# The scaling of differential attention's output, five copies of the embedding product, and the last gate's tile, moved in a two-layer encoder trunk

## The chip, the core and the metric

The kernel runs on one core of one Trainium2 chip. The metric is the device time of one execution in microseconds (us). TensorE is called PE below, its weight loads PEld, VectorE DVE, ScalarE ACT, GpSimd POOL, and SyncE, which issues the DMAs, SP.

## What is computed

A two-layer encoder over 1024 tokens of width 1024, float32. Layer 0 mixes tokens by neighbourhood attention, layer 1 by dense differential attention; each layer then has a gated feed-forward part and adds a sigmoid-gated embedding. Cut to what matters here:

```python
# layer 1, per head h and block of 128 queries
s = einsum('bhmqd,bhmkd->bhmqk', qb, k) + bias[None, :, None]   # two maps m = 0, 1
a = softmax(s, axis=-1)
w = a[:, :, 0] - lam_full * a[:, :, 1]
o = einsum('bhqk,bhkd->bhqd', w, v)
...
o = rms_norm(o, subln_g) * (1.0 - lambda_init)
...
# the end of each layer
gate = sigmoid(rms_norm(x, g[4]) @ ple_w_gate[i])
x = x + gate * (p[i] @ ple_w_proj[i])
```

## The kernel before, in words

Every float32 product is made of three matmuls of float32r parts (high by high, high by low, low by high). PE's order is written by hand. Only the differential attention (`da`) and the end of layer 1 are touched by the change.

**Differential attention.** There are 64 steps: 8 heads with 8 blocks of 128 queries. A turn `n` of the loop in `da` (L1193) issues on PE, in this order: the values of step n-1 (`da_values`, L1143), the scores of step n+1 for both maps (`da_scores`, L1088), the transposes of the weights of step n in two halves (`da_turn`, L1129), and the transpose of the scaled output of step n-1 (`da_out`, L1160). Between these, `tick` draws matmuls from a second stream (`da_stream`): the projections of later heads (L286 to L288), then the embedding product (`embed_steps`, L2146), then two blocks of the output projection (L1379).

Inside this loop the order of ACT, DVE and POOL is written by hand too: they run what the program issues, in that order. The chain beside PE for step n+1 is: DVE adds the bias to the scores of map 0 and takes the row's minimum (`biased`, L1099), then the same for map 1; ACT takes the exponential of map 0 and of map 1 (`da_exp`, L1106), each needing its minimum; DVE joins the two maps to weights (`da_weights`, L1113 to L1116); PE transposes these in the next turn, and ACT copies each half out of PSUM (L1132). For step n-1, whose values PE has just made, ACT squares and sums the output (L1146), DVE adds epsilon (L1147), POOL takes the power -0.5 (`root`, L298), and DVE scales the output by it (L1152), which PE then transposes (L1160). The tile `os` that the scaling writes has one buffer.

The second stream takes its PSUM banks from a pool of two (`take`, L611). The embedding product makes 16 tiles of 128x512; each is copied out of its bank by ACT (`evict`, L2154) and sent to DRAM by SP (L2155). PE can begin the next tile but one only when the copy has freed the bank. The copies are issued where `tick` happens to draw the tile's last unit: behind the exponential of map 0 (L1211), of map 1, or at the end of the turn.

**The last gate.** `embed` (L1998) makes, for each of 8 blocks of tokens, the product with `ple_w_gate` (24 matmuls of 128x512 for each half of 512 columns), and `gate` (L2025) takes the sigmoid on ACT (L2031), multiplies by the embedding and adds it to the residual on DVE (L2032, L2033), and sends the result off (L2034). For the last block of layer 1 PE makes one half after the other, and `gate` handles both halves after that. Both lie in one tile `g` of two banks.

## Time and profile before

| what | value |
|---|---|
| time, median of 3 runs | 2694.28 us (2693.45 to 2697.17) |
| the profiled execution's own time | 2693.09 us |
| its span, first to last instruction | 2691.3 us |
| PE busy | 2655.9 us, 99% |
| DVE, ACT, POOL busy | 1966.0, 1382.3, 549.4 us |
| granted TensorE clock | 1.00 |
| differential attention | about 1310 to 1885 us |

Durations below come from that one execution. Matmuls are pipelined: a matmul of 128x512 is shown 0.39 us long, though the next one starts 0.23 us later, so what counts on PE is the distance of the starts. A wait of an engine is shown as idle time before an instruction with the one that released it.

### The profile page before, as it was taken

The page shows a single profiled execution, that of the slowest core. Times are in us where ns is not written, and L with a number is a line of the kernel's source. Part 1 is how long each engine was busy: PE and PEld are TensorE (multiplying, and loading weights), DVE is VectorE, ACT ScalarE, POOL GpSimd, SP SyncE. Part 2 cuts the span into 40 slices and gives each one's busy share as a digit, 9 for nine tenths or more (in the row PEclk, how much of TensorE's full clock was granted, in tenths as well). Part 3 has the DMA queues.
Part 4 walks back from the last instruction along what each step waited for, and adds up shares of the span by engine and source line. Part 5 has one row for each costly group of instructions (what it writes and reads, how often), then busy time and mean ns, then how long its engine had stood idle before and what let it go on. Part 6 is the DMA issues. An engine that isn't in the chain of part 4 may idle for free.

```text
span 2691.3 us, 37010 instructions
## 1 busy us (share of the span) xinstructions
PE 2655.9 (99%) x13384; PEld 2195.3 (82%) x13384; DVE 1966.0 (73%) x3369; ACT 1382.3 (51%) x2612; POOL 549.4 (20%) x526
## 2 busy tenths in 40 slices
PE   8999999999999999999999999999999999999999
PEld 6888887878888888888778888877878888888887
DVE  5777776699777768666577777775798777767674
ACT  5555556454444444454466666675454343444452
POOL 2221220003333301001542122210103433300000
PEclk9999999999999999999999999999999999999999
DMA  6223226423322273343346555552413232373342
GB/s 185 85 66 105 77 94 192 136 67 122 118 101 111 91 277 137 110 130 121 123 155 211 202 174 200 180 180 92 157 65 142 84 117 94 122 262 123 117 138 101
DMA packets 150937, 360.91 MB, mean 134 GB/s; under 512 B 14137, under 2 KB 41017, under 8 KB 150754
## 3 DMA queue, kind: packets, MB, share of 16 engines
q1 hardware_dynamic: 150754, 358.56, 39.7%
q8 instruction: 105, 1.72, 0.3%
q14 instruction: 78, 0.64, 0.1%
HBM read 277.79 MB, written 92.90 MB: 138 GB/s over the span
## 4 chain that ended last, share of the span: by engine, by line
PE 84%; DVE 6%; ACT 3%; DMA 3%; issue 2%; POOL 1%; SPq 0%; DVEq 0%; ACTq 0%; POOLq 0%
PE b L286 19%; PE b L287 19%; PE b L288 19%; PE g L1379 6%; PE m L1379 5%; PE b L1143 3%; PE s L1088 3%; PE b L1129 2%; PE b L317 2%; PE b L1379 2%; PE av L981 2%; PE b L954 1%; DMA r<-in_ffn_w_out 1%; DVE r L252 1%; ACT E L1106 1%
## 5 line engine op out<-in xcount | busy, mean ns | idle before, releaser
L286 PE MATMUL b<-r,ws 128*128 128x512 f32 (+1 forms) x1308 | 532.8, 407 | 2.5 <-DVE r L421 1.8
L288 PE MATMUL b<-r,ws 128*128 128x512 f32 (+1 forms) x1308 | 506.2, 387 | 0.6 <-DVE ws L252 0.6
L287 PE MATMUL b<-r,ws 128*128 128x512 f32 (+1 forms) x1308 | 505.5, 386 | 0.7 <-DVE r L252 0.5
L288 PEld LDWEIGHTS b<-r,ws 128*128 128x128 f32 x1308 | 246.1, 188 | 53.1 <-DVE ws L252 1.8
L286 PEld LDWEIGHTS b<-r,ws 128*128 128x128 f32 x1308 | 246.8, 189 | 50.4 <-issue 3.3
L287 PEld LDWEIGHTS b<-r,ws 128*128 128x128 f32 x1308 | 247.6, 189 | 34.9 <-DVE r L252 1.9
L298 POOL TENSOR_TENSOR ss<-ss,mhalf 128x1 f32<-128x1 f32 x128 | 77.7, 608 | 953.8 <-DVE ss L1147 426.3
L286 PE MATMUL b<-r,wa 128*128 128x512 f32 x688 | 268.3, 390 | 2.0 <-DVE B L1772 2.0
L288 PE MATMUL b<-r,wa 128*128 128x512 f32 x688 | 268.2, 390 | 0.0
L287 PE MATMUL b<-r,wa 128*128 128x512 f32 x688 | 267.9, 389 | 0.0
L286 PE MATMUL b<-r,r 128*128 128x512 f32 x648 | 254.5, 393 | 1.0 <-ACT ws L2143 0.6
L287 PE MATMUL b<-r,r 128*128 128x512 f32 x648 | 252.9, 390 | 0.4 <-DVE r L252 0.3
L288 PE MATMUL b<-r,r 128*128 128x512 f32 x648 | 252.6, 390 | 0.0
L249 ACT ACTIVATE r<-raw 128x512 fp32r<-128x512 f32 (+1 forms) x168 | 109.0, 656 | 193.7 <-PE b L287 168.1
L252 DVE TENSOR_TENSOR ws<-raw,ws 128x512 fp32r<-128x512 f32 (+3 forms) x177 | 172.6, 981 | 45.0 <-ACT ws L249 43.2
L249 ACT ACTIVATE ws<-raw 128x512 fp32r<-128x512 f32 (+3 forms) x177 | 122.3, 697 | 108.4 <-PE b L288 52.0
L252 DVE TENSOR_TENSOR r<-raw,r 128x512 fp32r<-128x512 f32 (+1 forms) x168 | 125.5, 752 | 67.8 <-ACT r L249 64.8
L1106 ACT ACTIVATE E<-E,mn 128x1024 f32<-128x1024 f32 x128 | 146.8, 1147 | 28.4 <-DVE mn L1099 26.6
L1379 PE MATMUL m<-r,ws 128*128 128x512 f32 x672 | 157.5, 392 | 0.0
L1379 PE MATMUL g<-r,ws 128*128 128x512 f32 x672 | 155.8, 391 | 0.0
L286 PEld LDWEIGHTS b<-r,wa 128*128 128x128 f32 x688 | 129.2, 188 | 29.8 <-DVE B L1772 3.2
L288 PEld LDWEIGHTS b<-r,wa 128*128 128x128 f32 x688 | 129.2, 188 | 27.8 <-DVE wa L252 0.9
(223 smaller groups left out, 5432.9 us busy)
## 6 DMA issues: line engine op xcount, KB each, us to landing
r<-stashT SPq DMA_DIRECT2D x108, 512.0 KB, 4.8
raw<-in_w_in SPq DMA_DIRECT2D x86, 512.0 KB, 3.5
raw<-in_qkv SPq DMA_DIRECT2D x48, 512.0 KB, 4.3
spillS<-r SPq DMA_DIRECT2D x88, 256.0 KB, 2.7
r<-in_ffn_w_out SPq DMA_DIRECT2D x40, 512.0 KB, 6.8
raw<-spillS SPq DMA_DIRECT2D x40, 512.0 KB, 3.5
spillA<-B SPq DMA_DIRECT2D x66, 256.0 KB, 2.8
raw<-spillA SPq DMA_DIRECT2D x30, 512.0 KB, 3.7
```

The costliest lines, as they stand in the source:

```text
L249: return self.nc.scalar.activation(hi, src, AF.Copy).ins
L252: return self.nc.vector.tensor_tensor(out=lo, in0=src, in1=hi.bitcast(F32), op=ALU.subtract).ins
L286: mm(out, sta[0], mov[0], start=first, stop=False, skip_group_check=onto)
L287: mm(out, sta[0], mov[1], start=False, stop=False, skip_group_check=onto)
L288: mm(out, sta[1], mov[0], start=False, stop=last, skip_group_check=onto)
L298: self.nc.gpsimd.tensor_tensor(out=ss, in0=ss, in1=self.mhalf, op=ALU.pow)
L317: self.nc.tensor.transpose(t[:, k * P : k * P + P], h[:, c : c + P], self.ident)
L981: nc.tensor.matmul(out, V[:, kb, m], a[:, at : at + w].rearrange("p k t -> p (k t)"), start=g % 2 == 0 and i + z == 0, stop=g % 2 == 1 and ...
L1088: nc.tensor.matmul(s[m][:, w], A[o, a, q], A[o, b, w], start=z == 0, stop=z == 2)
L1106: self.exp = self.nc.scalar.activation(e, e, AF.Exp, bias=mn, scale=-1.0, accum_out=sm).ins
L1143: nc.tensor.matmul(o, wT[:, k], V[:, k], start=k == 0, stop=k == KT - 1)
L1379: mm(out[half], a, b[:, w], start=first and k + z == 0, stop=last and k == n - 1 and z == 2)
```

## The change

Three edits. In the attention, `da_values` no longer issues the scaling; it leaves it in `self.scaled`, and `da_scores` issues it between the biased scores of the two maps. `embed_steps` sets `self.last`, and from there on the exponential of map 0 is issued after the tick that follows it, so copies drawn in that tick come first. In `embed` the last block of layer 1 gets three separate banks, of 512, 256 and 256 columns, from two pools; `gate` is called after each part's matmuls. `times_steps` takes a part's own width.

```diff
@@ -856,7 +856,7 @@
     def begin(self, stream):
         self.stream, self.qk, self.v, self.credit, self.rate, self.open = stream, {}, {}, 0.0, 6, False
         self.heads, self.now, self.extra = {}, 0, 0
-        self.third = False
+        self.third = self.last = False
         self.jobs = []
 
     def tick(self, part):
@@ -1088,7 +1088,10 @@
                     nc.tensor.matmul(s[m][:, w], A[o, a, q], A[o, b, w], start=z == 0, stop=z == 2)
         a = (NT - 1 - t) * P
         e = [self.page(x, f"E{m}", bufs=2 - m) for m in range(2)]
-        mn = [self.biased(s[m], self.T[:, a : a + SEQ], e[m]) for m in range(2)]
+        mn = [self.biased(s[0], self.T[:, a : a + SEQ], e[0])]
+        self.scaled()
+        self.scaled = lambda: None
+        mn.append(self.biased(s[1], self.T[:, a : a + SEQ], e[1]))
         if h + 1 < D_HEADS:
             for c0, c1 in {3: ((1408, TW),), 6: ((1024, 1408),), 7: ((512, 1024), (0, 512))}.get(t, ()):
                 self.load_T(h + 1, c0, c1)
@@ -1149,7 +1152,11 @@
         if self.third:
             at = self.base
             self.slot("A", 1.3, at + 2.5), self.slot("D", 0.7, at + 2.7), self.slot("G", 4.3, at + 3.3)
-        nc.vector.tensor_scalar(out=os, in0=o, scalar1=r0, scalar2=r, op0=ALU.mult, op1=ALU.mult)
+
+        def scaled():
+            nc.vector.tensor_scalar(out=os, in0=o, scalar1=r0, scalar2=r, op0=ALU.mult, op1=ALU.mult)
+
+        self.scaled = scaled
         self.chunk[n] = b, os
 
     def da_out(self, x, n, oT):
@@ -1182,6 +1189,7 @@
             self.region = self.tc.manual_schedule(engines={ENG.Activation, ENG.DVE, ENG.Pool})
             self.region.__enter__()
             self.base = self.now
+            self.scaled = lambda: None
             self.da_scores(x, 0)
             self.da_exp(0, 0), self.da_exp(0, 1)
             self.tick(12 / 6)
@@ -1201,14 +1209,19 @@
                 if n + 1 < N:
                     self.need(self.qk, (n + 1) // NT)
                     self.da_scores(x, n + 1)
+                self.scaled()
+                self.scaled = lambda: None
                 if n == N:
                     self.drain()
                 if n < N:
                     self.da_turn(x, n, 0)
-                if n + 1 < N:
+                late = self.last
+                if n + 1 < N and not late:
                     self.da_exp(n + 1, 0)
                 self.now = self.base + 3.9
                 self.tick(0.34)
+                if n + 1 < N and late:
+                    self.da_exp(n + 1, 0)
                 if n < N:
                     self.da_turn(x, n, 1)
                 if n + 1 < N:
@@ -1375,7 +1388,7 @@
         for k, ((sh, sl), (wh, wl)) in enumerate(zip(sta, mov)):
             for z, (a, b) in enumerate(((sh, wh), (sh, wl), (sl, wh))):
                 for half in range(len(out)):
-                    w = slice(half * 512, half * 512 + 512)
+                    w = slice(half * 512, half * 512 + out[half].shape[-1])
                     mm(out[half], a, b[:, w], start=first and k + z == 0, stop=last and k == n - 1 and z == 2)
                 if z == 0:
                     yield
@@ -2022,12 +2035,12 @@
             hi, lo = part[t] = [self.page(self.ws, "ws", (P, KT, P), F32R) for _ in range(2)]
             self.transposed(h[t], lambda g, ps: self.split(ps, hi[:, 4 * g : 4 * g + 4], lo[:, 4 * g : 4 * g + 4]), pool)
 
-        def gate(t, o):
+        def gate(t, o, parts=None):
             f = f_acc[t]
-            e[t] = self.page(self.raw, "raw")
-            nc.sync.dma_start(e[t], self.pp[layer][rows[t]])
-            halves = (slice(0, 512), slice(512, D))
-            for o, w in zip(o, halves) if len(o) == 2 else ((o[0], slice(0, D)),):
+            if e[t] is None:
+                e[t] = self.page(self.raw, "raw")
+                nc.sync.dma_start(e[t], self.pp[layer][rows[t]])
+            for o, w in zip(o, parts or ((slice(0, 512), slice(512, D)) if len(o) == 2 else (slice(0, D),))):
                 opened.append(nc.scalar.activation(o, o, AF.Sigmoid).ins)
                 nc.vector.tensor_tensor(out=e[t][:, w], in0=e[t][:, w], in1=o, op=ALU.mult)
                 nc.vector.tensor_tensor(out=f[:, w], in0=f[:, w], in1=e[t][:, w], op=ALU.add)
@@ -2060,17 +2073,22 @@
                 if t == 0:
                     o = None
                     two = [self.bank(self.pj) for _ in range(2)]
+                elif last and t == NT - 1:
+                    two = [self.bank(self.pj), self.bank()[:, :256], self.bank(self.pj)[:, :256]]
                 else:
                     o = pg.tile([P, D], F32, tag="g", name=self.uid("g"))
                     two = [o[:, :512], o[:, 512:]]
                 hi, lo = part[t]
                 sta = [(hi[:, k], lo[:, k]) for k in range(KT)]
                 if last and t == NT - 1:
-                    for n, half in enumerate((slice(0, 512), slice(512, D))):
-                        self.times(two[n : n + 1], sta, [(a[:, half], b[:, half]) for a, b in W])
+                    self.times([two[0]], sta, [(a[:, :512], b[:, :512]) for a, b in W])
+                    gate(t, two[:1], (slice(0, 512),))
+                    for n, w in enumerate((slice(512, 768), slice(768, D))):
+                        self.times([two[1 + n]], sta, [(a[:, w], b[:, w]) for a, b in W])
+                        gate(t, two[1 + n : 2 + n], (w,))
                 else:
                     self.times(two, sta, W)
-                gate(t, two if o is None or last and t == NT - 1 else [o])
+                    gate(t, two if o is None else [o])
                 if 0 < t < NT - 2:
                     residual(t + 2)
                 if t > 0 and not last:
@@ -2145,6 +2163,7 @@
 
     def embed_steps(self, layer, a, b):
         nc, pages = self.nc, {}
+        self.last = True
 
         def evict(t, half, o):
             at = t % 2 * 512
```

On DVE, one step of the attention with the embedding product beside it (L1152 the scaling, the pairs L1099 the biased scores of map 0 and map 1 with their minima, `ss` the sum of squares). Before:

```order
L1147 TENSOR_SCALAR ss_16446<-ss_16446 128x1
L252 TENSOR_TENSOR r_2598_16308<-r_2599_16309,r_2597_16307 128x1024
L1152 TENSOR_SCALAR os_16445<-b_2626_16436,sum_16280,ss_16446 128x128
L1099 ISA E_2631_16467,mn_16469<-s_16453,T_11298 128x1024
L1099 ISA mn_16469 128x1
L1099 ISA E_2632_16468,mn_16471<-s_16454,T_11298 128x1024
L1099 ISA mn_16471 128x1
```

The same place after the change (the line numbers move: L1147 is L1150, L1152 is L1157, L1099 is L1102):

```order
L1150 TENSOR_SCALAR ss_16446<-ss_16446 128x1
L252 TENSOR_TENSOR r_2598_16308<-r_2599_16309,r_2597_16307 128x1024
L1102 ISA E_2631_16466,mn_16468<-s_16452,T_11298 128x1024
L1102 ISA mn_16468 128x1
L1157 TENSOR_SCALAR os_16445<-b_2626_16436,sum_16280,ss_16446 128x128
L1102 ISA E_2632_16467,mn_16471<-s_16453,T_11298 128x1024
L1102 ISA mn_16471 128x1
```

The scaling has gone from ahead of both maps to between them; this holds for 62 of the 64 steps, and in the last two, with no scores behind them, nothing moves. No other instruction of DVE in the attention changes its place.

On ACT, the same step (L1132 the copies of the transposed weights, L1106 the exponentials of map 0 and 1, L2154 the copy of an embedding tile, L249 the high part of a split). Before:

```order
L249 ACTIVATE r_2597_16307<-r_2599_16309 128x1024
L1132 ACTIVATE wT_16475<-b_2638_16476 128x512
L1106 ACTIVATE E_2631_16467,sum_16473<-E_2631_16467,mn_16469 128x1024
L2154 ACTIVATE ws_16486<-b_2625_16432 128x512
L1132 ACTIVATE wT_16475<-b_2641_16493 128x512
L1106 ACTIVATE E_2632_16468,sum_16474<-E_2632_16468,mn_16471 128x1024
```

After (L1135 is the copy of the weights, L1109 the exponential, L2173 the embedding's copy):

```order
L249 ACTIVATE r_2597_16307<-r_2599_16309 128x1024
L1135 ACTIVATE wT_16475<-b_2638_16476 128x512
L2173 ACTIVATE ws_16485<-b_2625_16432 128x512
L1109 ACTIVATE E_2631_16466,sum_16473<-E_2631_16466,mn_16468 128x1024
L1135 ACTIVATE wT_16475<-b_2641_16493 128x512
L1109 ACTIVATE E_2632_16467,sum_16474<-E_2632_16467,mn_16471 128x1024
```

The embedding's copy now stands ahead of the exponential of map 0. Five of the 16 copies move in this way; the others keep their places. PE's order differs only in the last block of the last gate, POOL's nowhere. On SP the gate's three transfers stand where two stood, and a few loads and stores of the attention swap places with their neighbours.

## The prediction

> **What bounds the kernel now.** I read the page first: TensorE (PE) is busy 99% of the span, so the kernel can get faster only where PE stands still, or behind PE's last matmul. The table of 50-us stretches says where it stands still. Its columns are the stretch, its length, then busy time and instruction count of PE, PEld, DVE, ACT, POOL.
>
> ```profile
> 1800.00:1850.00 50.00, 45.02 (x284) 35.67 (x281) 36.17 (x67) 36.40 (x73) 4.98 (x6) 1.00 0.38 128
> ```
>
> This is the stretch of the differential attention that is emptiest on PE: 5.0 us are missing, while no other engine is near full. So it is a matter of order, not of load. Next the waits from 1320 to 1890 us, the whole of that attention (who waited for whom: total us, times, longest):
>
> ```profile
> DVE os L1152 <- POOL ss L298: 30.2, 47, 0.7
> ACT E L1106 <- DVE mn L1099: 23.8, 35, 2.4
> PE b L286 <- ACT ws L2154: 4.0, 3, 2.0
> PE b L1129 <- DVE E L1116: 0.8, 1, 0.8
> PE b L286 <- DVE r L194: 0.5, 1, 0.5
> PE b L286 <- DVE r L198: 0.3, 1, 0.3
> ```
>
> The largest wait of PE is for L2154, the copies of the embedding product out of PSUM. VectorE's 30 us of waiting for GpSimd's power (L298) before the scaling (L1152) is large but hardly reaches PE: it delays the biased scores (L1099), these the exponentials (L1106), and only three small waits of PE (0.8, 0.5, 0.3) come from work behind them.
>
> The timeline around the longest wait, all engines (start, length, engine, line; in brackets the idle time before and its releaser):
>
> ```profile
> 1798.78 1.65 PE L1088 MATMUL s<-r 64*128 64x512 f32 x12
> ...
> 1800.66 1.22 DVE L252 TENSOR_TENSOR r<-r,r 128x1024 fp32r<-128x1024 f32 x1
> ...
> 1801.31 0.40 PE L288 MATMUL b<-r,proj 128*128 128x512 f32 x1
> 1801.38 0.61 ACT L1132 ACTIVATE wT<-b 128x512 f32<-128x512 f32 x1
> ...
> 1802.65 1.22 DVE L1099 CUSTOM_DVE_ANT_0 E<-s,T 128x1024 f32<-128x1024 f32 x1
> ...
> 1803.36 0.27 PE L1160 MATMUL b<-ident,os 128*128 128x128 f32 x1
> ...
> 1803.91 1.15 ACT L1106 ACTIVATE E<-E,mn 128x1024 f32<-128x1024 f32 x1 [1.91 <-DVE mn L1099]
> ...
> 1805.05 0.58 ACT L2154 ACTIVATE ws<-b 128x512 f32<-128x512 f32 x1
> ...
> 1805.68 0.50 PE L286 MATMUL b<-r,v 128*128 128x512 f32 x1 [2.05 <-ACT ws L2154]
> ```
>
> PE finished the bank at 1801.31 + 0.40 = 1801.71. ScalarE was free at 1801.99, but the next in its queue is the exponential, which waits 1.91 us for VectorE. The copy stands behind it and starts at 1805.05, and PE gets the bank at 1805.68.
>
> **The change part by part.** *Copies ahead of exponentials.* Five copies swap places with the first exponential of a step; nothing is added. In the step above the copy can run at 1802.0 and end by 1802.6, before PE needs the bank: the whole stall goes, 1805.68 - 1803.36 = 2.32 us between the two PE starts. The other stalls of the kind:
>
> ```profile
> 1817.72 1.66 PE L1088 MATMUL s<-r 64*128 64x512 f32 x12
> ...
> 1820.01 1.22 DVE L1099 CUSTOM_DVE_ANT_0 E<-s,T 128x1024 f32<-128x1024 f32 x1
> ...
> 1824.66 0.50 PE L286 MATMUL b<-r,v 128*128 128x512 f32 x1 [1.10 <-ACT ws L2154]
> ...
> 1833.09 0.50 PE L286 MATMUL b<-r,v 128*128 128x512 f32 x1 [0.87 <-ACT ws L2154]
> ...
> 1839.68 0.39 PE L288 MATMUL b<-r,proj 128*128 128x512 f32 x1
> ...
> 1841.77 0.50 PE L1379 MATMUL b<-r,ws 128*128 128x512 f32 x1 [0.91 <-ACT ws L2154]
> ```
>
> The idle time in brackets counts from a matmul's modelled end, 0.39 us after its start, while a stream starts one every 0.23 us (worked out below), so each stall is 0.16 longer than its bracket. The one at 1833.09 goes whole: 0.87 + 0.16 = 1.0. At 1841.77 the bank's last matmul ends only at 1839.68 + 0.39 = 1840.07; the copy runs to about 1840.65 and PE goes on at 1840.7, 1.05 earlier. The copy before 1824.66 is not swapped (it stands behind the second exponential), so it gains only what the scores gain: they were complete at 1817.72 + 1.66 = 1819.38 and the biased scores started at 1820.01, so 0.6. Sum 2.3 + 1.0 + 1.05 + 0.6 = 4.95; between 2.5 (half of it) and 5.8 (all four stalls).
>
> The price of this is an exponential behind a copy whose bank is not full yet, as in the last case: the scores' chain loses up to 0.6 us there, of which most comes back, since the copy no longer stands between the two exponentials. I put it at nothing; the bound is 0.6 in each of the five places.
>
> *Scaling between the two maps.* VectorE's queue keeps its instructions; in 62 steps the scaling goes behind the first biased scores. An ordinary step, same columns:
>
> ```profile
> 1513.21 1.67 PE L1088 MATMUL s<-r 64*128 64x512 f32 x12
> ...
> 1514.63 0.41 DVE L1152 TENSOR_SCALAR os<-b,sum,ss 128x128 f32<-128x128 f32 x1
> ...
> 1514.95 1.22 DVE L1099 CUSTOM_DVE_ANT_0 E<-s,T 128x1024 f32<-128x1024 f32 x1
> ...
> 1516.09 1.22 DVE L1099 CUSTOM_DVE_ANT_0 E<-s,T 128x1024 f32<-128x1024 f32 x1
> ...
> 1516.21 1.15 ACT L1106 ACTIVATE E<-E,mn 128x1024 f32<-128x1024 f32 x1
> ...
> 1517.13 0.27 PE L1160 MATMUL b<-ident,os 128*128 128x128 f32 x1
> ...
> 1517.84 1.14 ACT L1106 ACTIVATE E<-E,mn 128x1024 f32<-128x1024 f32 x1
> ```
>
> Here the scores are there at 1514.88 and the first biased scores start at 1514.95: moving the scaling gains 0.05 for the first map and puts the second one 1516.09 - 1514.95 = 1.14, plus 0.32 for the scaling, behind 1514.90: 1516.36 instead of 1516.09. It ends at 1517.58, and its exponential starts at 1517.84 in any case, since ScalarE is busy until then. The scaling itself ends at 1514.90 + 1.14 + 0.41 = 1516.45 instead of 1515.04, and its transpose on PE (L1160) comes at 1517.13: 0.7 us of cover. So an ordinary step gains and loses nothing. A step in which VectorE waits for GpSimd is another thing: at 1802.65 the scores had been complete since 1800.43 and VectorE was free at 1801.88, so 0.77 us are gained, at most the wait's mean 30.2 / 47 = 0.64 plus 0.32. The three waits of PE behind that chain (0.8, 0.5, 0.3, each 0.16 longer) are each under that: they can go whole, 2.1, or stay, 0; I take 1.7, since the wait behind them is as long as they are.
>
> The price: where PE's transpose comes soon after, it waits. At 1803.36 it comes 0.07 before the new end of the scaling, 1801.88 + 1.14 + 0.41 = 1803.43. That and VectorE's work behind the second map, 0.27 later in ordinary steps, I put at 0.3 in all, 0 to 2. Attention: 4.95 + 1.7 - 0.3 = 6.35, from 2.5 to 7.9.
>
> *Last gate's tile.* The end of the timeline:
>
> ```profile
> 2662.71 22.02 PE L1379 MATMUL g<-r,ws 128*128 128x512 f32 x96
> ...
> 2673.89 1.01 ACT L2031 ACTIVATE g<-g 128x1024 f32<-128x1024 f32 x1 [9.77 <-PE g L1379]
> 2674.93 1.22 DVE L2032 TENSOR_TENSOR raw<-raw,g 128x1024 f32<-128x1024 f32 x1 [8.22 <-ACT g L2031]
> ...
> 2684.77 0.58 ACT L2031 ACTIVATE g<-g 128x512 f32<-128x512 f32 x1 [9.87 <-PE g L1379]
> 2685.38 0.69 DVE L2032 TENSOR_TENSOR raw<-raw,g 128x512 f32<-128x512 f32 x1 [7.97 <-ACT g L2031]
> ...
> 2687.44 0.69 DVE L2033 TENSOR_TENSOR facc<-facc,raw 128x512 f32<-128x512 f32 x1
> ```
>
> PE ends at 2684.73, VectorE at 2688.13: 3.40 us, because neither half's sigmoid starts before the whole tile is done. After it only the last 256 columns hang on PE's end. By the rows of 1024 and 512 columns a sigmoid of 256 takes 0.58 - 0.43 / 2 = 0.365, each of the two VectorE steps 0.69 - 0.53 / 2 = 0.425: with the gaps of 0.03 or so seen here 1.31. PE has 48 matmuls of 256 columns for 24 of 512. The 96 take 22.02, so one starts every (22.02 - 0.39) / 95 = 0.228; for 256 columns the first and the last of 23 consecutive matmuls in the entry stage:
>
> ```profile
> 34.49 0.28 PE L287 MATMUL b<-r,ws 128*128 128x256 f32 x1
> ...
> 37.12 0.28 PE L288 MATMUL b<-r,ws 128*128 128x256 f32 x1
> ```
>
> That is 2.63 / 22 = 0.120 each, weight load included. 48 x 0.120 - 24 x 0.228 = 0.29, less 0.11 for the shorter last matmul (0.28 for 0.39): 0.2 later. The last transfer is half as large:
>
> ```profile
> out<-facc SPq DMA_DIRECT2D x4, 512.0 KB, 2.9
> out<-facc SPq DMA_DIRECT2D x2, 256.0 KB, 2.0
> ```
>
> So it lands in 2.0 at most, 1.55 if the line goes on; I take 0.2 off. The end: 3.40 - 1.31 - 0.2 + 0.2 = 2.1 earlier, from 1.9 to 2.35.
>
> One rule speaks against the narrow matmuls. The Trainium skill (TensorE: Matmul & The Clock Gate, Packing small matmuls) says that a weight load overlaps a matmul in flight only when their row groups differ; as an estimate from that page's figures a pair would then take 107 + 109 = 216 ns and the 48 of them 10.4 us. The trace does not agree: 0.120 a pair.
>
> **Sum.** 6.35 + 2.1 = 8.45. The profiled execution took 2693.09, so 2684.6 by its clock; the median of the runs is 1.19 higher, which gives 2685.8.
>
> **The rivals.** *The wait only moves.* A bank set free earlier meets the next wait: PE's transpose for the scaling, or a copy that waits for its own bank. For it: at 1803.36 the cover is already used up, and one of the four stalls is bound by the bank. Against it: ScalarE and VectorE are busy 36 of 50 us there. Half the copies' stalls and nothing else of the attention: 2.5 + 2.1 - 0.3 = 4.3, 2690.0. Chance 0.15.
>
> *The second map sets the step.* The scaling now stands between the two maps and costs 0.32 in each of 62 steps, 19.8 us, if the second exponential and the weights behind it (L1116) are what PE waits for; then only copies and end are gained, 7.05: 2693.09 + 19.8 - 7.05 + 1.19 = 2707.0. It decides from where the second exponential starts within 0.27 of its minimum. Against it: in the ordinary step 0.26 of cover is left after the move, and PE waited for L1116 once in the whole attention. For it: that cover is thin. Chance 0.04.
>
> *Narrow matmuls as dear as wide ones.* If the pace is set by the weight load, the 24 additional pairs cost 0.228 each, 5.5 instead of 0.29: 5.2 less gain, 2691.0. The rows say 0.120. This is what the rule above would do here. Chance 0.01.
>
> **How the numbers follow.** Forecast 0.80, at 2685.8. Its own range comes from the bounds: the most is 7.9 + 2.35 = 10.25 (2684.0), the least 2.5 + 1.9 = 4.4 (2689.9), which is already the first rival's ground. To leave out no more than 2 in 10 the range reaches to the first rival, and a little under the most for the runs' own spread (2693.45 to 2697.17 before): 2683.4 to 2690.2. About 0.2%, 5.4 us, is what a measurement of this kernel tells from no change. Gains over that, below 2688.9, are the forecast: 0.80. Within it lie the first and third rival: 0.16. Slower is the second: 0.04.
>
> **What would show it.** Right: no PE wait for the embedding copies over 1 us, the stretch 1800 to 1850 with 48 or more busy on PE, VectorE's wait for L298 before the scaling near nothing, 1.3 to 1.6 us between PE's last matmul and VectorE's last add, 256-column matmuls 0.12 apart. Wrong: new PE waits at L1160 for the scaling, or at L1129 for the weights, that add up to several us; a second exponential that waits for its minimum in most steps; a copy that waits for PE with an exponential behind it for longer than 0.6.

## The result, and the profile after

| kernel | median, us | range, us | runs |
|---|---|---|---|
| before | 2694.84 | 2693.45 to 2697.17 | 6 |
| after | 2682.69 | 2682.26 to 2684.36 | 6 |

The ratio is 0.9955, with a 95% interval of 0.9942 to 0.9968: the change gains 12.15 us, where 8.45 was forecast, and the time lies 0.7 us below the range. The profiled execution of after took 2682.94 us, its span is 2681.1 (before: 2691.3), so by the two profiles the gain is 10.2 us.

In after the lines of the program have moved: the biased scores are L1102 (before L1099), the exponentials L1109 (L1106), the weights L1119 (L1116), their transposes L1132 (L1129), the values L1146 (L1143), the scaling L1157 (L1152), its transpose L1167 (L1160), the copies L2173 (L2154).

The table of stretches for after, with the columns as before: the stretch that was emptiest on PE has 49.26 of 50 us busy, where it had 45.02.

```profile
1800.00:1850.00 50.00, 49.26 (x315) 39.70 (x316) 36.98 (x71) 37.54 (x76) 4.13 (x6) 1.00 0.39 125
```

The waits of after from 1320 to 1890 us (total, times, longest):

```profile
DVE E L1102 <- PE s L1088: 32.4, 52, 1.0
...
ACT E L1109 <- DVE mn L1102: 5.3, 9, 1.7
...
DVE os L1157 <- POOL ss L298: 1.5, 2, 0.7
...
PE b L1167 <- DVE os L1157: 1.3, 2, 1.0
...
PE b L286 <- ACT ws L2173: 0.5, 1, 0.5
```

VectorE's 30.2 us of waiting for GpSimd's power have become 1.5. It now waits 32.4 us for PE's scores: it is ready before them, in 52 steps. ScalarE's wait for the minimum fell from 23.8 to 5.3, PE's wait for the copies from 4.0 to 0.5. PE waits 1.3 for the scaled output; 1.0 of that stood there before, in the last step.

The timeline of after at the place of the stall that was the longest (it had ended at 1805.68):

```profile
1798.42 0.62 ACT L2173 ACTIVATE ws<-b 128x512 f32<-128x512 f32 x1
...
1799.49 0.41 DVE L1157 TENSOR_SCALAR os<-b,sum,ss 128x128 f32<-128x128 f32 x1
...
1799.61 1.15 ACT L1109 ACTIVATE E<-E,mn 128x1024 f32<-128x1024 f32 x1 [0.57 <-DVE mn L1102]
...
1799.95 0.33 PE L1167 MATMUL b<-ident,os 128*128 128x128 f32 x1
...
1800.04 0.48 PE L286 MATMUL b<-r,v 128*128 128x512 f32 x1
```

The copy runs ahead of the exponential and is done at 1799.04; PE goes on at 1800.04 with no bracket. What PE waits for now is the scaling: it ends at 1799.90 and PE's transpose starts at 1799.95, which is 0.40 us behind the start of the matmul ahead of it and not the usual 0.23. These 0.17 us are too short to get a bracket.

The end of after's timeline:

```profile
2669.66 7.27 PE L1392 MATMUL b<-r,ws 128*128 128x512 f32 x54
...
2676.96 0.37 ACT L2044 ACTIVATE b<-b 128x256 f32<-128x256 f32 x1 [2.51 <-PE b L1392]
2677.36 0.42 DVE L2045 TENSOR_TENSOR raw<-raw,b 128x256 f32<-128x256 f32 x1 [2.00 <-ACT b L2044]
2677.82 0.42 DVE L2046 TENSOR_TENSOR facc<-facc,raw 128x256 f32<-128x256 f32 x1
```

PE ends at 2676.93 and VectorE at 2678.24: 1.31 us, as worked out ahead (before: 3.40). What is left of the span behind it is 2.86 us, 0.31 less than before.

Where the 10.2 us of the spans come from can be read off four starts, the first and the last scores of the attention and one between. Of before, then of after:

```profile
1308.53 1.66 PE L1088 MATMUL s<-r 64*128 64x512 f32 x12
...
1861.31 1.66 PE L1088 MATMUL s<-r 64*128 64x512 f32 x12
```

```profile
1308.91 1.66 PE L1088 MATMUL s<-r 64*128 64x512 f32 x12
...
1795.12 1.64 PE L1088 MATMUL s<-r 64*128 64x512 f32 x12
...
1853.36 1.66 PE L1088 MATMUL s<-r 64*128 64x512 f32 x12
```

From the first scores to the last: 552.78 us before, 544.45 after, 8.33 less. The prediction's step at 1798.78 came 490.25 us behind the first scores; the same step now comes 486.21 behind them. So 4.04 us are gained ahead of the stretch in which copies stand behind exponentials, where only the scaling was moved, and 4.29 in and behind it. From the last scores to PE's end 0.15 us is lost, the narrow matmuls' part of it included, and behind PE's end 2.40 is gained (6.57 to 4.17); the attention starts 0.38 later. 8.33 + 2.40 - 0.15 - 0.38 = 10.2.

### The profile page after: what moved, and what is told of

The parts are those of the page before. It is cut to its first block, busy times and chain, and to the rows that moved or that the text cites. A ratio compares the mean times of both kernels' runs of the same rounds, so it can differ in the third digit from the quotient of the medians.

```text
span 2681.1 us, 37009 instructions
## 1 busy us (share of the span) xinstructions
PE 2654.3 (99%) x13408; PEld 2196.4 (82%) x13408; DVE 1964.9 (73%) x3371; ACT 1383.4 (52%) x2613; POOL 549.7 (21%) x526
## 4 chain that ended last, share of the span: by engine, by line
PE 89%; DVE 4%; DMA 2%; ACT 2%; issue 1%; POOL 1%; SPq 0%; ACTq 0%; DVEq 0%; POOLq 0%
PE b L286 20%; PE b L288 20%; PE b L287 20%; PE m L1392 5%; PE g L1392 5%; PE b L1146 4%; PE s L1088 4%; PE b L1132 2%; PE b L1392 2%; PE b L317 2%; PE av L981 2%; PE b L954 1%; DMA r<-in_ffn_w_out 1%; DMA x<-in_x 1%; DVE r L252 1%
## 5 line engine op out<-in xcount | busy, mean ns | idle before, releaser
L249 ACT ACTIVATE r<-raw 128x512 fp32r<-128x512 f32 (+1 forms) x168 | 109.0, 656 | 193.4 <-PE b L287 168.9
L252 DVE TENSOR_TENSOR ws<-raw,ws 128x512 fp32r<-128x512 f32 (+3 forms) x177 | 171.2, 973 | 44.8 <-ACT ws L249 42.7
L1102 DVE CUSTOM_DVE_ANT_0 E<-s,T 128x1024 f32<-128x1024 f32 x128 | 155.7, 1218 | 33.6 <-PE s L1088 32.4
L249 ACT ACTIVATE ws<-raw 128x512 fp32r<-128x512 f32 (+3 forms) x177 | 122.4, 698 | 108.8 <-PE b L288 52.0
L252 DVE TENSOR_TENSOR r<-raw,r 128x512 fp32r<-128x512 f32 (+1 forms) x168 | 124.5, 746 | 70.2 <-ACT r L249 67.3
L1109 ACT ACTIVATE E<-E,mn 128x1024 f32<-128x1024 f32 x128 | 146.9, 1148 | 9.6 <-DVE mn L1102 8.0
```

The lines of the kernel that those rows point to most:

```text
L249: return self.nc.scalar.activation(hi, src, AF.Copy).ins
L252: return self.nc.vector.tensor_tensor(out=lo, in0=src, in1=hi.bitcast(F32), op=ALU.subtract).ins
L1102: self.nc.vector.tensor_tensor_reduce(out=e, in0=s, in1=bias, scale=1.0, scalar=3e38, op0=ALU.add, op1=ALU.min, accum_out=mn)
L1109: self.exp = self.nc.scalar.activation(e, e, AF.Exp, bias=mn, scale=-1.0, accum_out=sm).ins
```

## The experiments

Theory A: the scaling's move is worth far more than the three waits by which it was priced, because it takes VectorE's wait for the power out of the chain that everything else hangs on; the copies' stalls are shortened by both edits. Theory B: the scaling is worth the 1.4 us forecast, and the rest comes from the edits acting together, or from the times of single executions. The length of the attention below is the start of the last scores less that of the first; in two executions of before it differs by 0.10 us, in two of after by 0.07. The row of after is measured against its own six runs of before (2694.84), the others against 24.

| kernel | median, us | ratio to before (95%) | attention, us | less than before |
|---|---|---|---|---|
| before | 2694.95 (24 runs) | 1 | 552.78 | |
| scaling alone | 2686.40 | 0.9970 (0.9958 to 0.9981) | 545.43 | 7.35 |
| copies alone | 2691.12 | 0.9986 (0.9977 to 0.9995) | 550.40 | 2.38 |
| tile alone | 2692.90 | 0.9995 (0.9986 to 1.0003) | 552.74 | 0.04 |
| no wait for the power | 2686.14 | 0.9968 (0.9957 to 0.9980) | 546.19 | 6.59 |
| after | 2682.69 | 0.9955 (0.9942 to 0.9968) | 544.45 | 8.33 |

**Scaling alone.** The kernel before with this part of the change, and with the scaling left in `self.scaled` by `da_values` as there:

```diff
-        mn = [self.biased(s[m], self.T[:, a : a + SEQ], e[m]) for m in range(2)]
+        mn = [self.biased(s[0], self.T[:, a : a + SEQ], e[0])]
+        self.scaled()
+        self.scaled = lambda: None
+        mn.append(self.biased(s[1], self.T[:, a : a + SEQ], e[1]))
```

> The kernel before with the scaling between the two maps and nothing else. Theory A (the traces of before and after: steps start 2.5 us earlier by step 37 and about 4.1 in all where only the scaling can act; VectorE's wait for GpSimd's power is out of its queue, and many small stalls of PE go, those of 0.2 to 0.3 us too): 3.5 to 4.5 us less than before, the sum of VectorE's waits for L298 ahead of the scaling under 3 us instead of 30. Theory B (the prediction's term, 1.7 - 0.3): 1.0 to 1.8 us less, the rest of the gain needs the other two edits beside it.

Measured: 8.55 us less by the medians, 7.35 in the attention's length. That is above what either theory said, since both had counted only the gain ahead of the copies. Its timeline shows the rest (starts of the four matmuls that wait for copies, and the first copy with its exponential; the copies are L2164 here):

```profile
1799.29 1.15 ACT L1109 ACTIVATE E<-E,mn 128x1024 f32<-128x1024 f32 x1 [0.84 <-DVE mn L1102]
...
1800.44 0.58 ACT L2164 ACTIVATE ws<-b 128x512 f32<-128x512 f32 x1
...
1801.07 0.51 PE L286 MATMUL b<-r,v 128*128 128x512 f32 x1 [0.69 <-ACT ws L2164]
...
1819.46 0.50 PE L286 MATMUL b<-r,v 128*128 128x512 f32 x1 [0.52 <-ACT ws L2164]
...
1827.04 0.50 PE L286 MATMUL b<-r,v 128*128 128x512 f32 x1
...
1835.13 0.50 PE L1389 MATMUL b<-r,ws 128*128 128x512 f32 x1 [0.32 <-ACT ws L2164]
```

The copy still stands behind the exponential. But the exponential no longer waits 1.91 us for its minimum, only 0.84, and the four brackets of PE (2.05, 1.10, 0.87, 0.91 before) have become 0.69, 0.52, none and 0.32. The step at 1798.78 came at 1795.50 here, 486.24 behind the first scores at 1309.26: 4.01 us are gained ahead of the copies and 3.34 at them, without a copy moved. More than half of the stalls that the prediction put down to the copies' place came from the scaling ahead of the scores, passed on by the minimum and the exponential.

**Copies alone.**

```diff
-                if n + 1 < N:
+                late = self.last
+                if n + 1 < N and not late:
                     self.da_exp(n + 1, 0)
                 self.now = self.base + 3.9
                 self.tick(0.34)
+                if n + 1 < N and late:
+                    self.da_exp(n + 1, 0)
```

> The kernel before with the five copies ahead of the exponentials and nothing else. Theory A (parts add up): 4.0 to 4.6 us less, from the stretch 1800 to 1850 alone, and the stalls of 0.3 to 0.9 us before 1800 us stay. The prediction's term: 4.95 less. Theory C (the copies' gain depends on the scaling's earlier scores): under 3.5 us, with one of the four stalls for L2154 still over 1 us.

Here `self.last` is set as in the change, and nothing else of it is taken.

Measured: 3.83 us less by the medians, which is above theory C's 3.5 and below theory A's 4.0, but 2.38 in the attention, which is all that the edit touches. One stall behind a copy is longer than 1 us, as theory C said (the last row below). The step at which before had its longest stall, in this kernel's timeline, and that row (the copies are L2158):

```profile
1802.67 0.62 ACT L2158 ACTIVATE ws<-b 128x512 f32<-128x512 f32 x1
...
1804.71 1.15 ACT L1106 ACTIVATE E<-E,mn 128x1024 f32<-128x1024 f32 x1 [1.43 <-DVE mn L1099]
...
1805.86 0.57 ACT L1132 ACTIVATE wT<-b 128x512 f32<-128x512 f32 x1
...
1806.49 1.72 PE L1143 MATMUL b<-v,wT 128*128 128x128 f32 x13 [0.80 <-ACT wT L1132]
...
1824.51 0.50 PE L286 MATMUL b<-r,v 128*128 128x512 f32 x1 [1.52 <-ACT ws L2158]
```

The copy is done in time and PE's wait for it is gone. But the exponential still waits for the minimum, and the next in ScalarE's queue, the copy of the transposed weights (L1132), stands behind it now: PE waits 0.80 for that. PE's order is the same in both kernels, so its matmuls can be compared start by start: the places at 1805.68, 1833.09 and 1841.77 of before gain 2.30, 1.12 and 1.01 us, about as forecast (2.3, 1.0, 1.05). The one at 1824.66 loses 0.43, and the new waits for L1132 cost 1.04 behind the first place and 0.49 behind the last. For the copies alone the first rival, the wait that only moves, took nearly half of the gain. The two edits are worth 7.35 + 2.38 = 9.73 us apart and 8.33 together: beside the scaling the copies' move is worth 0.98, beside the copies the scaling is worth 5.95.

**The last gate's tile alone.** The part of the diff in `gate`, `embed` and `times_steps`.

> The kernel before with the last gate's tile in three banks and nothing else. Theory A and the prediction: 1.9 to 2.35 us less, 1.3 to 1.6 us from PE's last matmul to VectorE's last add. If the time outside the span also shrinks with this edit (the medians of before and after differ by 2 us more than the spans): 3 to 4 us less by the medians, while the span is only 2.1 shorter.

Measured: 2.05 us less by the medians, which the interval does not tell from no change, and 1.3 by the spans (2690.0 for 2691.3), below the 1.9 that was expected. Behind PE's last matmul the span has 4.2 us left, as in after, and not 6.6 as in before: 2.4 are gained there. But from the last scores to PE's end this execution took 1.2 longer than that of before. About 0.3 of that are the narrow matmuls; the rest lies in the feed-forward stage, where executions of one kernel differ too (the last runs below). So the chain shows the tile's gain, and the total does not.

**No wait for the power.** The scaling stays ahead of both maps, but its second factor is a column that is long there. The factor of the RMS norm is left out of what this kernel computes.

```diff
-        nc.vector.tensor_scalar(out=os, in0=o, scalar1=r0, scalar2=r, op0=ALU.mult, op1=ALU.mult)
+        nc.vector.tensor_scalar(out=os, in0=o, scalar1=r0, scalar2=self.neglam, op0=ALU.mult, op1=ALU.mult)
```

> The kernel before, with the scaling in its old place but multiplied by lambda's column (written long before) in place of GpSimd's power: it leaves the factor of the RMS norm out, so its output is not the reference's. VectorE no longer waits for GpSimd. Theory A (the wait is what the scaling's old place cost): 3 to 4.5 us less than before, about as the scaling's move alone. Theory D (what matters is that the first biased scores no longer stand behind 0.41 us of scaling): under 1 us less.

Measured: 8.81 us less by the medians, 6.59 in the attention, nine tenths of what the move alone gives. Its waits, 1320 to 1890 us, and the stall that was the longest in before:

```profile
ACT E L1106 <- DVE mn L1099: 7.5, 8, 1.8
...
PE b L1129 <- DVE E L1116: 0.7, 1, 0.7
```

```profile
1800.70 0.50 PE L286 MATMUL b<-r,v 128*128 128x512 f32 x1 [1.04 <-ACT ws L2154]
```

ScalarE's wait for the minimum fell from 23.8 to 7.5, nearly as in after (5.3), though the scaling is still ahead of the scores. So it is mostly the wait that costs, not the 0.41 us of scaling. Theory D falls, and theory A is shown in its main point, though the gain is above its bound of 4.5. The stall of 2.05 is 1.04 here and 0.69 with the scaling moved: about half of it was the wait for the power. The place itself is worth the other 0.76. This kernel keeps the wait of 0.7 for L1116, which the kernel with the scaling alone has not; that one has a new wait of PE for the scaled output in its place, which takes half of it back. The remaining 0.4 or so lie at the copies.

**Scaling behind both maps.** The kernel after, with the scaling one place later:

```diff
-        mn = [self.biased(s[0], self.T[:, a : a + SEQ], e[0])]
+        mn = [self.biased(s[m], self.T[:, a : a + SEQ], e[m]) for m in range(2)]
         self.scaled()
         self.scaled = lambda: None
-        mn.append(self.biased(s[1], self.T[:, a : a + SEQ], e[1]))
```

> The kernel after with the scaling behind the biased scores of both maps, 1.14 us later. Theory A (the place between the maps is the latest that PE's transpose L1167 bears: its cover was worked out as 0.7 us in an ordinary step): PE waits 0.4 to 0.5 us for os in most of 62 steps, 15 to 31 us more than after. Theory E (any place behind the first biased scores does, since only VectorE's wait for the power mattered): within 1 us of after.

Measured: 2692.65 us, ratio to before 0.9992 (0.9983 to 1.0001), 9.96 more than after; the attention is 553.44, 8.99 longer. Its waits (the scaling is L1156, its transpose L1166):

```profile
PEld b L1166 <- DVE os L1156: 15.6, 24, 1.4
...
PE b L1166 <- DVE os L1156: 6.5, 14, 1.0
```

The direction is theory A's and theory E falls, but the size is below A's bound of 15: PE's weight load waits for the scaled output in 24 steps, not in most of 62. The cover of 0.7 us in the step that the prediction showed is less than most steps have: in after the median from the scaling's end to its transpose is 1.35, above the 1.14 by which it was moved here. Still, the later place takes back all that the whole change gives in the attention.

**Scaling twice.** The kernel after, with a second scaling into a tile that nobody reads:

```diff
+        os2 = self.page(x, "os2", (P, P), bufs=1)
         def scaled():
+            nc.vector.tensor_scalar(out=os2, in0=o, scalar1=r0, scalar2=r, op0=ALU.mult, op1=ALU.mult)
             nc.vector.tensor_scalar(out=os, in0=o, scalar1=r0, scalar2=r, op0=ALU.mult, op1=ALU.mult)
```

> The kernel after with the scaling done twice between the maps, once into a tile that nobody reads, so 0.32 us more ahead of the second map. The prediction's second rival (the second map sets the step; 0.26 us of cover is left): if it is right that this cover is there, 0.06 us in most steps, 1 to 5 us more than after; if the cover had been used up already, 0.32 in 62 steps, up to 20 us more; if much more cover is there than the ordinary step shows, under 1 us.

Measured: 2688.67 us, ratio 0.9978 (0.9970 to 0.9987), 5.98 more than after; the attention is 6.01 longer. That is just above the 1 to 5 of the case with cover and far from 20. It does not come from the second exponential. Its waits (transpose L1170, scaling L1160), and the dearest of them in the timeline:

```profile
PE b L1170 <- DVE os L1160: 2.7, 4, 1.3
...
PE b L288 <- DVE ws L252: 1.8, 2, 1.4
...
PE b L286 <- DVE r L182: 0.6, 1, 0.6
```

```profile
1344.42 2.28 DVE L252 TENSOR_TENSOR ws<-raw,ws 128x1024 fp32r<-128x1024 f32 x1
...
1346.76 0.50 PE L288 MATMUL b<-r,ws 128*128 128x512 f32 x1 [1.42 <-DVE ws L252]
```

PE waits for the scaled output and for VectorE's work behind the second map for the second stream (L252, L182), and nowhere for the weights (L1119). So the second rival's mechanism was not at work; the prediction's price of 0.3 names the right waits, PE's transpose and "VectorE's work behind the second map", and a second scaling makes them cost 6. The dearest is not a sum of small delays: L252 takes 2.28 us here and 1.23 in after, where it starts ahead of a GpSimd instruction and not behind it (the last section).

**Two banks.** The kernel after, with the last gate's tile as two banks of 512 columns:

```diff
-                    two = [self.bank(self.pj), self.bank()[:, :256], self.bank(self.pj)[:, :256]]
+                    two = [self.bank(self.pj), self.bank()]
...
-                    for n, w in enumerate((slice(512, 768), slice(768, D))):
+                    for n, w in enumerate((slice(512, D),)):
```

> The kernel after with the last gate's tile in two banks of 512 columns, no 256-column matmuls. By the rows: the last chain on ACT and VectorE is 0.58 + 0.69 + 0.69 with gaps, 2.06 instead of 1.31, PE ends 0.2 earlier, the last transfer lands up to 0.2 later: 0.5 to 1.0 us more than after, and 1.1 to 1.6 less than with both halves behind the whole tile. If narrow matmuls cost more than 0.12 us a pair: no slower than after.

Measured: 2683.97 us, 1.28 more than after by the medians, a little above the 0.5 to 1.0 expected, and 1.0 by the spans (2682.1), of which 0.26 lies in the attention. The end of its timeline:

```profile
2669.69 7.19 PE L1392 MATMUL b<-r,ws 128*128 128x512 f32 x31
...
2676.91 0.58 ACT L2044 ACTIVATE b<-b 128x512 f32<-128x512 f32 x1 [4.86 <-PE b L1392]
2677.53 0.69 DVE L2045 TENSOR_TENSOR raw<-raw,b 128x512 f32<-128x512 f32 x1 [4.03 <-ACT b L2044]
2678.25 0.69 DVE L2046 TENSOR_TENSOR facc<-facc,raw 128x512 f32<-128x512 f32 x1
```

From PE's end at 2676.88 to the last add's at 2678.94 it is 2.06 us, as expected, against 1.31. The last 24 matmuls of 512 columns lie between the two halves' sigmoids (2671.47 and 2676.91): 5.44 us; the 48 of 256 columns in after took from 2671.21 to 2676.96, 5.75. So the narrow ones cost 0.3 more and 5.75 / 48 = 0.120 each. The rule of the Trainium skill (TensorE: Matmul & The Clock Gate, Packing small matmuls), by which the prediction had 216 ns a pair, differs from this, and the measurement decides.

**A version beyond both.** The kernel after, with the second exponential and the weights, too, behind the tick that follows while the embedding product runs, and with the three units of the second stream that PE did ahead of the last values left for behind them:

```diff
-                if n == N:
-                    self.tick(0.6)
...
-                    self.da_exp(n + 1, 1)
+                    if not late:
+                        self.da_exp(n + 1, 1)
...
-                    self.da_weights(n + 1)
+                    if not late:
+                        self.da_weights(n + 1)
                 self.now = self.base + 5.8
                 self.tick(0.16)
+                if n + 1 < N and late:
+                    self.da_exp(n + 1, 1)
+                    self.da_weights(n + 1)
```

> The kernel after with the second exponential and the weights, too, issued behind the tick that follows them while the embedding product runs, and the 3 units of the second stream that PE did ahead of the last values left for behind them. Theory A (what is left in the trace of after: 0.69 us at 1818 for a copy behind the second exponential, 1.17 us at the last step, where PE has too little left to do): 1.2 to 1.9 us less than after. Rival (the wait only moves: the weights or the transposed halves come later instead, L1132 or L1146 wait): the last step's 1.17 is gained, the 0.69 comes back elsewhere, 0.5 to 1.2 less.

Measured: 2681.34 us (2679.78 to 2682.38), ratio to before 0.9949 (0.9937 to 0.9962); 1.35 below after's median, though the two intervals overlap. The attention is 0.61 shorter, and in the last step the stall of after is gone. The row of after, and then that of this kernel with the scaling ahead of it:

```profile
1872.41 0.33 PE L1167 MATMUL b<-ident,os 128*128 128x128 f32 x1 [1.01 <-DVE os L1157]
```

```profile
1868.84 0.41 DVE L1157 TENSOR_SCALAR os<-b,sum,ss 128x128 f32<-128x128 f32 x1 [0.73 <-POOL ss L298]
...
1869.95 0.27 PE L1167 MATMUL b<-ident,os 128*128 128x128 f32 x1
```

Both parts do what theory A said, 0.61 and the 1.01 of the bracket, and the medians' 1.35 lies in its range, but runs that overlap can't tell it from the rival's 1.2. In the profiled execution one wait in the feed-forward stage behind it was 1.1 longer than in after's (PE for VectorE's L252, 1.5 for 0.4). The edit does not touch that stage, and unchanged kernels differ there too, as the next runs show, though by less.

**Second profiles of before and after.** Both kernels unchanged.

> The kernel before, unchanged, for a second profile. By the medians the change gains 12.1 us, by the two profiled executions 10.2. If the first profile of before caught a short execution (its own time, 2693.09, lies below all but two of the runs that were timed), this one is 1 to 2 us longer, the attention the same within 0.1 us, and the difference lies in the entry and the feed-forward stages, where PE waits for VectorE. If not: 2693 again, and the change gains something outside the span.

> The kernel after, unchanged, for a second profile: 2682.3 to 2684.4 us, the attention within 0.1 us of the first profile, differences of up to 1 us in the entry and the feed-forward stages as in the kernel before.

Measured: 2693.71 and 2682.62 us, 11.1 apart. The attention's lengths are 552.68 and 544.52, within 0.1 of the first profiles. The wait of PE for VectorE in the feed-forward stage, in the waits from 2300 to 2690 us of the first profile of before and of the second:

```profile
PE b L287 <- DVE r L252: 0.3, 1, 0.3
```

```profile
PE b L287 <- DVE r L252: 1.0, 2, 0.7
```

So executions of one kernel differ by waits there. The second execution of before is 0.6 longer than the first, less than the 1 to 2 that were expected, and it is still 1.2 below the median of the 24 runs. The time outside the span explains none of it: in every execution on record, of whatever kernel, the time is 1.7 to 1.9 us above the span. The median span of the 24 runs of before is 2693.2 and that of after's six 2680.9. So the whole gain of about 12 us lies between the first and the last instruction, and the first profile of before was a short execution; which waits are longer in the executions without a profile was not seen.

## Why the prediction was right in direction and too small

**The copies, 4.95.** In the place where these were counted 4.29 us were gained, by both edits. Start by start, before against after, the four places gain 2.24, 0.60, 1.12 and 1.00, which is 4.96. What is missing is mostly the price that was put at nothing: at 1832.74 of after the embedding's copy waits 0.73 for PE, with the exponential and the copy of the transposed weights behind it, and PE loses 0.45 (the row at 1835.01 below). That is the last of the prediction's signs of being wrong, and the loss lies within its bound of 0.6. Another 0.27 is lost around the transpose at 1799.95, most of it to the scaling. The step holds for the whole, not in its attribution, and that the sum came so near is partly luck: the copies' move gives 2.38 alone and 0.98 beside the scaling. The prediction saw the chain (the copy behind an exponential that waits 1.91 us for VectorE), and it took the queue's order as the cause; the other end of the same chain, the wait for the power, is the larger one.

**The scaling, 1.7 - 0.3.** This is the step that failed: 1.4 was forecast, and it is 4.04 us ahead of the copies' stretch, and 7.35 as an edit by itself. The prediction took "the three waits of PE behind that chain (0.8, 0.5, 0.3)" for all that 30 us of VectorE's waiting do to PE, from the list of waits. These three did go, and gained 0.80, 0.77 and 0.45, about the 2.1 that it gave them at most. The rest of the 4.04, and 0.5 more that a new wait takes back, come from places that it did not name: 2.5 us. Its list is short in three ways. The timeline of before shows two:

```profile
1661.49 0.40 PE L288 MATMUL b<-r,ws 128*128 128x512 f32 x1
...
1661.95 0.50 PE L286 MATMUL b<-r,ws 128*128 128x512 f32 x1
1662.29 0.39 PE L287 MATMUL b<-r,ws 128*128 128x512 f32 x1
...
1686.47 0.40 PE L288 MATMUL b<-r,ws 128*128 128x512 f32 x1
...
1687.04 0.50 PE L286 MATMUL b<-r,ws 128*128 128x512 f32 x1 [0.17 <-ACT r L190]
...
1687.37 0.40 PE L287 MATMUL b<-r,ws 128*128 128x512 f32 x1
```

At 1661.95 PE starts 0.46 us after the last matmul, twice the usual 0.23, with no bracket: the gap lies almost wholly in the modelled end of a matmul of 0.40. A stall of up to 0.3 us is in no list of waits. By the starts four of this kind in before, at 1374, 1391, 1601 and 1661 us, of 0.23 to 0.29 each, hang on the scaling: all four are still there with the copies alone. With the scaling alone and in after three are gone, and the one at 1601 is 0.1 shorter. (Others of 0.22, ahead of the transposes of the weights, stay in every kernel.) At 1687.04 the bracket says 0.17; the distance of the starts is 0.57 instead of 0.23, 0.34 lost, and the next start comes after 0.33, 0.10 more. So a bracket of 0.17 stands for 0.44. The prediction added the 0.16 of the modelled end, not the 0.1 of the restart. Third, the four stalls at the copies were named by their last releaser, L2154, though the scaling's wait stood three links back: with that wait alone taken out their brackets fall from 4.93 to 2.22.

**The price, 0.3.** Small, as forecast, but twice as large by the starts as by the list. Two rows of after, the new wait for the scaled output and the late copy of the transposed weights:

```profile
1371.86 0.33 PE L1167 MATMUL b<-ident,os 128*128 128x128 f32 x1 [0.27 <-DVE os L1157]
...
1835.01 1.16 PE L1146 MATMUL b<-v,wT 128*128 128x128 f32 x8 [0.18 <-ACT wT L1135]
```

The bracket at 1371.86 says 0.27, and against before 0.45 is lost there; another 0.16 is lost at 1799.95. That makes 0.6, inside the 0 to 2 that the prediction allowed (and left out of its lowest sum for the attention, 2.5). VectorE's later work behind the second map does not show in after. How near it is, the kernels with the scaling later or twice tell: 9 and 6 us more.

**The tile, 2.1.** Right in each term: 1.31 for the chain, 0.3 for the narrow matmuls (0.2 forecast), 0.31 for the transfer (0.2 forecast).

**The median, 1.19 above the execution.** By the same measure, span against span, 8.45 was forecast and 10.2 measured. The other 1.9 of the 12.15 are the offset: before's median was 1.75 above its profiled execution, after's 0.25 below. An offset taken from three runs and one profiled execution, and carried over to another kernel, was off by 1.9 us here, and the prediction had left 0.6 for it (2684.0 to 2683.4). These 1.9 us lie inside the span, as the runs' spans show; in which stage is open. It took both misses to leave the range: with the scaling's 2.6 us more or with these 1.9 alone the time would have been inside it.

**The rivals.** The wait that only moves takes nearly half of what the copies' move gains by itself; beside the scaling it takes 0.45, since the minimum comes early enough. The second map did not set the step. Narrow matmuls cost 0.120 each.

## What to carry to other kernels

When an engine waits often and briefly in a chain that others hang on, don't price the move that removes it by the last engine's listed waits: follow each stall of the busy engine back through all its links, and compare distances of starts with the usual one. Two edits that shorten the same stall can't be added; name for each stall which edit is enough alone. A wait that is moved behind one piece of ready work can cost nothing there, but one place further it can cost as much as it gained, so its cover has to be read in many steps, not in one.

## What the runs showed of the hardware

A first matmul of 512 columns behind a stall is longer than the next ones: the second starts 0.33 to 0.34 us after it and not 0.23 (the rows at 1661.95 and 1687.04 above). It need not be the stall itself: behind the four short transposes of a step the second one comes after 0.31 to 0.32, though PE did not wait. In both cases the first one's weight load starts with it or less than 0.1 us ahead, and in the stream 0.23 ahead, which would explain it; no run here tested that.

VectorE's work on two operands in SBUF is longer when GpSimd is already at work. Of the 64 instructions that make the weights (L1116) in before, the 58 beside which no GpSimd instruction ran took 1.26 or 1.27 us. The other six began 0.05 to 0.17 us behind the start of a `tensor_tensor` of GpSimd and took 2.18 to 2.32. One of them, with three such instructions of 1.3 us each, the last of which overlaps it:

```profile
1363.85 3.90 POOL L707 TENSOR_TENSOR r<-r,r 128x512 f32<-128x512 f32 x3
...
1366.52 2.32 DVE L1116 SCALAR_TENSOR_TENSOR E<-E,c,E 128x1024 f32<-128x1024 f32 x1
```

That is part of the wait of 0.8 for L1116: in after it takes 2.19 in this step, but starts early enough for PE. Where VectorE began first, with L252 at 1344.36 in before, it kept its 1.22 us and GpSimd's instruction took 2.30. The Trainium skill (SBUF — State Buffer, SBUF: two separate sides) says that the two engines share a pair of ports under an exclusive lock, so that the later one stands still until the other's instruction ends. The trace agrees, as far as its spans of GpSimd go: in these rows the one that begins later is the longer, by 0.9 to 1.1 us, which is less than one instruction of the other. The power looks like such a case: it takes 0.55 us in most steps, and 0.86 to 1.40 in the eight in which VectorE waited 0.44 for it, each with an L252 of VectorE beside it. At 1800.89 in before it began 0.23 us behind L252 and took 1.40, so VectorE's wait of 0.44 for it in that step, by the same reading, came from VectorE's own work.
